# Three mixers of a transformer: the exact rest of each weight computed on GpSimd instead of VectorE

## The chip, the cores and the metric

One core of one Trainium2 chip runs the whole program. The metric is the device time of one execution in microseconds; of several executions of a kernel the median is taken. TensorE (PE) multiplies matrices, VectorE (DVE), ScalarE (ACT) and GpSimd (POOL) work on tiles elementwise, and SyncE (SP) and GpSimd start transfers from HBM.

## The reference

Two transformer blocks on 256 tokens of width 1024, all in float32. What is computed around the change is the hybrid mixer, run twice (once for each layer of the first block), and a third mixer with sparse attention, a state-space branch and memory attention in the second block:

```python
def hybrid_mixer(x, w_in, mix_scale, w_out, ...):
    proj = jnp.einsum('btd,de->bte', x, w_in)
    (a_q, a_k, a_v, a_decay, a_beta, a_gate, c_glu, f_q, f_k, f_v, f_forget) = split_columns(proj, IN_SIZES)
    ...
    o_a = gated_delta_rule(heads(a_q, GDN_HEADS), heads(a_k, GDN_HEADS), heads(a_v, GDN_HEADS), log_decay, beta)
    ...

def gated_delta_rule(q, k, v, g, beta):
    '''Chunked gated delta rule.
    S_t = exp(g_t) * S_{t-1} (I - beta_t k_t k_t^T) + beta_t k_t v_t^T ;  o_t = S_t^T q_t
    ...

def first_block(x, ...):
    for l in range(DEPTH):
        mix = hybrid_mixer(x, w_in[l], ...)
        x = layer_norm(DEEPNORM_ALPHA * x + mix, ln_mix_g[l], ln_mix_b[l])
        if l % 2 == 0:
            ff = swiglu(x, ffn_w1[l // 2], ffn_w3[l // 2], ffn_w2[l // 2])
        else:
            ff = moe_swiglu(x, moe_router[l // 2], moe_w1[l // 2], moe_w3[l // 2], moe_w2[l // 2])
        x = layer_norm(DEEPNORM_ALPHA * x + ff, ln_ffn_g[l], ln_ffn_b[l])
    return x
```

The mixer joins three branches: the gated delta rule (a solve in each chunk of 64 tokens, then a scan over four chunks), a depthwise convolution of 31 taps over a gated unit with a norm and a sigmoid behind it, and a forgetting attention. Their outputs are scaled, joined to 1024 columns and multiplied by `w_out`.

## The kernel before, in words

Seven stages run one after the other: mixer 1 (layer 0), a dense feed-forward, mixer 2 (layer 1, the same code), a mixture of experts, a feed-forward, mixer 3 (the second block's mixer), and a last feed-forward. A stage opens its PSUM banks with `banks(...)`, whose tags name how many banks each use has. The three mixers, and they alone, have the tags `a=2, g=4, f=2`.

Dense products are made of three fast matmuls instead of one slow one. `load` (line 162) has SP bring 128 x 2048 raw weights into one of four buffers. `part` (line 169) cuts them into parts of 1024 columns. For each part ACT writes the rounded half `wh` (line 172), and VectorE the exact rest `wl`, raw minus rounded (line 174). Each has three buffers. `mm3` (lines 182 to 185) multiplies high by high, high by low and low by high. A part feeds 24 matmuls in the mixers. `proj_a` and `proj_b` are the two forms of projection, with the activations on one side or the other; in the trace their outputs are `a_pA`, which reads `wl` in line 185, and `a_pB`, which reads it in line 184. A raw buffer is free for the next load once both halves are made.

A scheduler that simulates the program's times sets the order of the instructions on all engines; each engine then works through its own list in order. In a mixer, code written later has lower priority. After the projections that the gated delta rule needs come the inverse of the 16 x 16 blocks (`invert16`, lines 509 to 513, on VectorE), `invert32`, `solve`, the scan (line 713 is its subtraction on VectorE, lines 721, 728 and 730 its state), the attention `fox` (line 661 is the maximum over its scores, line 683 its output), the convolution and the gates, in the order of the call `self.emit(inverse(), scan(), fox(), conv(), gates())`. The generators are merged by the scheduler. `spare(c)` (line 612) makes a projection tile that one of them asks for.

The convolution `conv` (line 740) makes its gated input `cup` (line 748). It has two halves of 128 channels. In layer 0 six taps of each go to TensorE as matmuls with diagonal weights (`a_conv`, 12 in all), and the other 25 to VectorE, where the first is a multiplication (line 762) and the rest are 48 multiply-adds (line 764) in the tile `ccv`. The trace counts a float32 matmul as two. Line 765 adds both. Then come a mean (`f_cmean`), a variance (`f_cvar`), the norm (lines 771 to 781), the sigmoid, and line 803, which splits the result for the output projection `w_out`. That projection is made in four column blocks, each over all 1024 rows, and the rows of the convolution are the fourth and fifth eighth of the first block already. Line 792 makes the gate, lines 812 to 816 the norm of the scan's output, line 278 the split of the other rows, line 826 the sum with the residual.

GpSimd only starts transfers before the change (28 instructions in all), such as the constants at the start and the two rows of each norm (`load_rows`, line 286).

Of the kernel before, what the change touches and what calls it, by code (L numbers as in the profile page):

```python
# [9 lines left out]
F32 = mybir.dt.float32  # L10
# [5 lines left out]
ALU = mybir.AluOpType  # L16
# [87 lines left out]
class Net:  # L104
# [64 lines left out]
    def part(self, raw, o=0, m=1024):  # L169
        nc = self.nc  # L170
        wh = self.wp.tile([P, 1024], F32R, name="wh")
        nc.scalar.activation(wh[:, :m], raw[:, o:o + m], AF.Copy)  # L172
        wl = self.wp.tile([P, 1024], F32R, name="wl")
        nc.vector.tensor_tensor(wl[:, :m], raw[:, o:o + m], wh[:, :m].bitcast(F32), op=ALU.subtract)  # L174
        return wh[:, :m], wl[:, :m]

    def weights(self, src, n=2048):
# [9 lines left out]
    @contextmanager  # L187
    def banks(self, **tags):

        with self.tc.tile_pool(name="ps", bufs=1, space=bass.MemoryType.PSUM, reuse_waits="tile") as pool:  # L190
            self.pp, self.tags = pool, tags
            yield

    def ps(self, tag, name):
# [1714 lines left out]
```

## Time and profile before

| what | value |
|---|---|
| median of 3 runs | 2217.02 us |
| the runs | 2215.6, 2217.02, 2223.44 us |
| the profiled execution | 2220.2 us |
| its span in the profile | 2218.4 us |
| mean granted TensorE clock | 0.963 |
| busy share of the span | PE 93%, DVE 58%, ACT 46%, POOL 1% |

The profile is one execution. Busy time is the union of an engine's instructions. "Wait" rows name the instruction that came last before the engine went on. Windows count from the start of the span, and the granted clock of a window is a share of full speed (2.4 GHz). The stages stand at 0 to 201 us (mixer 1), 201 to 430 (feed-forward), 430 to 634 (mixer 2), 634 to 1600 (mixture of experts), 1600 to 1786 (feed-forward), 1786 to 2012 (mixer 3) and from 2012 (last feed-forward). A name such as `wl<-raw,wh` is the tile written and the tiles read.

### The profile page before, as it was taken

To read this page: it belongs to the slowest core of one execution; us is meant where nothing else is said; L and a number is where in the kernel's file an instruction comes from. 1 tells how busy PE (TensorE), PEld (TensorE's weight loads), DVE (VectorE), ACT (ScalarE), POOL (GpSimd) and SP (SyncE) were. 2 spreads that over 40 slices of the span, in tenths; PEclk is the share of its full clock that TensorE was granted. 3 is DMA by queue.
4 is the path that set the end of the run, shared out by engine and by line. 5 is a ranking of instruction groups with operands and counts; after the bars stand their busy time and mean duration, and the time that the engine had idled before them with its cause. 6 is when DMAs were issued, how large, how long until landed. Compare 5 with 4: busy or idle time off the path is not lost. (4 is left out here: it accounts for less than half of the span.)

```text
span 2218.4 us, 31878 instructions
## 1 busy us (share of the span) xinstructions
PE 2061.1 (93%) x12770; PEld 1609.1 (73%) x12770; DVE 1294.1 (58%) x1903; ACT 1023.4 (46%) x1448; POOL 14.6 (1%) x28
## 2 busy tenths in 40 slices
PE   8998959899979999998899999988699999999998
PEld 7878949788768888533368786332599988878997
DVE  6768925567659898410178985000554568665454
ACT  6545414465437777400167774000444444554443
POOL 0000000000000000000000000000000000000000
PEclk9979979999789999999999999999799999999999
DMA  6313797433158999799999999999555553344552
GB/s 231 105 39 135 213 105 292 160 115 106 72 214 315 350 346 349 307 425 425 426 425 425 355 343 358 425 425 424 193 178 187 188 196 128 133 150 153 184 188 96
DMA packets 80059, 548.31 MB, mean 247 GB/s; under 512 B 9392, under 2 KB 11696, under 8 KB 15008
## 3 DMA queue, kind: packets, MB, share of 16 engines
q1 hardware_dynamic: 75888, 527.40, 63.0%
q0 software_dynamic: 4016, 18.79, 4.2%
q8 instruction: 103, 1.69, 0.3%
q14 instruction: 52, 0.43, 0.1%
HBM read 536.72 MB, written 9.43 MB: 246 GB/s over the span
## 5 line engine op out<-in xcount | busy, mean ns | idle before, releaser
L174 DVE TENSOR_TENSOR wl<-raw,wh 128x1024 fp32r<-128x1024 f32 (+1 forms) x662 | 798.8, 1218 | 411.8 <-ACT wh L172 408.5
L172 ACT ACTIVATE wh<-raw 128x1024 fp32r<-128x1024 f32 (+1 forms) x662 | 693.9, 1055 | 629.9 <-PE a_pA L184 255.2
L183 PE MATMUL a_pA<-xTh,wh 128*128 128x256 f32 x1456 | 419.8, 289 | 26.0 <-ACT wh L172 22.3
L185 PE MATMUL a_pA<-xTh,wl 128*128 128x256 f32 x1456 | 416.0, 286 | 1.2 <-DVE wl L174 1.2
L184 PE MATMUL a_pA<-xTl,wh 128*128 128x256 f32 x1456 | 415.9, 286 | 0.0
L183 PEld LDWEIGHTS a_pA<-xTh,wh 128*128 128x128 f32 x1456 | 281.4, 194 | 34.8 <-ACT wh L172 23.2
L184 PEld LDWEIGHTS a_pA<-xTl,wh 128*128 128x128 f32 x1456 | 281.4, 193 | 4.5 <-issue 3.2
L185 PEld LDWEIGHTS a_pA<-xTh,wl 128*128 128x128 f32 x1456 | 281.1, 193 | 4.5 <-issue 2.2
L1032 PE MATMUL a_up<-raw,xef 128*64 128x512 f32 x896 | 218.7, 597 | 26.2 <-DMA raw<-in_moe_w_dram 26.2
L1037 DVE TENSOR_TENSOR mos<-mos,a_up 128x512 f32<-128x512 f32 x42 | 28.7, 682 | 267.4 <-PE a_up L1032 258.5
L184 PE MATMUL a_up<-wl,xeh 128*128 128x512 f32 x448 | 180.3, 402 | 1.9 <-DVE wl L174 1.8
L1032 PEld LDWEIGHTS a_up<-raw,xef 128*64 128x64 f32 x896 | 68.5, 136 | 154.8 <-issue 106.2
L185 PE MATMUL a_up<-wh,xel 128*128 128x512 f32 x448 | 178.0, 397 | 0.0
L183 PE MATMUL a_up<-wh,xeh 128*128 128x512 f32 x448 | 175.7, 399 | 0.0
L183 PE MATMUL a_pB<-wh,xTh 128*128 128x256 f32 x480 | 140.8, 295 | 5.7 <-ACT glu L620 3.2
L1065 PE MATMUL y_y<-raw,mof 128*64 128x512 f32 x448 | 133.4, 608 | 7.4 <-DMA raw<-in_moe_w_dram 7.3
L185 PE MATMUL a_pB<-wh,xTl 128*128 128x256 f32 x480 | 138.3, 291 | 1.5 <-DVE xTl L278 1.5
L184 PE MATMUL a_pB<-wl,xTh 128*128 128x256 f32 x480 | 139.2, 291 | 0.0
L184 PEld LDWEIGHTS a_up<-wl,xeh 128*128 128x128 f32 x448 | 84.7, 189 | 28.3 <-DVE wl L174 6.8
L1036 ACT ACTIVATE mos<-a_up 128x512 f32<-128x512 f32 x42 | 24.7, 587 | 170.8 <-PE a_up L1032 168.6
L184 PE MATMUL acc_acc<-wl,ffh 128*128 128x512 f32 x264 | 102.9, 395 | 0.5 <-DVE wl L174 0.5
L185 PE MATMUL acc_acc<-wh,ffl 128*128 128x512 f32 x264 | 102.7, 395 | 0.0
(559 smaller groups left out, 2772.2 us busy)
## 6 DMA issues: line engine op xcount, KB each, us to landing
raw<-in_moe_w_dram SPq DMA_DIRECT2D x336, 1024.0 KB, 10.6
raw<-in_ffn_in_dram SPq DMA_DIRECT2D x44, 1024.0 KB, 4.9
raw<-in_ffn_w_dram SPq DMA_DIRECT2D x33, 1024.0 KB, 5.0
raw<-in_w_in_a_dram SPq DMA_DIRECT2D x24, 1024.0 KB, 4.9
raw<-in_ffn_out_dram SPq DMA_DIRECT2D x22, 1024.0 KB, 4.9
raw<-in_w_out_dram SPq DMA_DIRECT2D x12, 1024.0 KB, 4.9
raw<-in_w_in_g_dram SPq DMA_DIRECT2D x12, 1024.0 KB, 5.0
raw<-in_w_in_b_dram SPq DMA_DIRECT2D x6, 1024.0 KB, 5.0
```

Of the source, the lines that this page charges most:

```text
L172: nc.scalar.activation(wh[:, :m], raw[:, o:o + m], AF.Copy)
L174: nc.vector.tensor_tensor(wl[:, :m], raw[:, o:o + m], wh[:, :m].bitcast(F32), op=ALU.subtract)
L183: mm(out, lh, rh, start=start, stop=False, skip_group_check=True)
L184: mm(out, lh, rl, start=False, stop=False, skip_group_check=True)
L185: mm(out, ll, rh, start=False, stop=stop, skip_group_check=True)
L1032: PE.matmul(ps[r], xe[0][:, k0, r], w[:, k * 512:k * 512 + 512], start=k0 == 0, stop=k0 == 7, skip_group_check=True)
L1036: self.last = S.activation(s, pp[0], AF.Silu)
L1037: V.tensor_tensor(s, s, pp[1], op=ALU.mult)
L1065: PE.matmul(py[h][r], hf[:, k, r], w[:, j * 1024 + h * 512:j * 1024 + h * 512 + 512], start=b == 0 and k == 0, stop=b == 6 and k == 3, ski ...
```

## The change

In the three mixers the subtraction of line 174 is issued on GpSimd instead of VectorE. The engine is chosen when the banks are opened: a stage with the tag `f` takes GpSimd, and the others keep VectorE. 123 of the 662 subtractions move: 34 in mixer 1 (one of 144 columns), 34 in mixer 2 (one of 144) and 55 in mixer 3 (one of 544). One line is added, so all lines behind 191 have a number higher by one.

```diff
         wl = self.wp.tile([P, 1024], F32R, name="wl")
-        nc.vector.tensor_tensor(wl[:, :m], raw[:, o:o + m], wh[:, :m].bitcast(F32), op=ALU.subtract)
+        self.rest.tensor_tensor(wl[:, :m], raw[:, o:o + m], wh[:, :m].bitcast(F32), op=ALU.subtract)
         return wh[:, :m], wl[:, :m]
...
         with self.tc.tile_pool(name="ps", bufs=1, space=bass.MemoryType.PSUM, reuse_waits="tile") as pool:
             self.pp, self.tags = pool, tags
+            self.rest = self.nc.gpsimd if "f" in tags else self.nc.vector
             yield
```

The scheduler then sets another order on every engine. On GpSimd, the start of the program, mixer 1 and the beginning of mixer 2 read as follows (`memd`, `biasd`, `rot` and `kept` are transfers of the feed-forward stage; `rows` are those of the norms):

```order
L174 ISA
L174 TENSOR_TENSOR wl<-raw,wh 128x144
L174 TENSOR_TENSOR wl<-raw,wh 128x1024 x28
L287 DMA rows<-in_ln_mix_dram 128x2048
L1366 DMA mem<-in_mem_dram 128x2048
L1387 DMA rb<-in_rel_bias_dram 32x8
L1388 DMA bk<-in_buckets_dram 32x512
L174 TENSOR_TENSOR wl<-raw,wh 128x1024 x5
...
L174 TENSOR_TENSOR wl<-raw,wh 128x144
L174 TENSOR_TENSOR wl<-raw,wh 128x1024
L287 DMA rows<-in_ln_ffn_dram 128x2048
```

The subtractions stand between the transfers that GpSimd issued before: the loads for the next stage are behind 29 of mixer 1's, and the load of the norm's rows in mixer 2 is behind the first two. In front of the first subtraction stands one instruction of another kind.

VectorE before, in mixer 1, from the attention's second half to the convolution's sum (`late` and `old` are the scan's tiles, `fsx` the attention's):

```order
L764 SCALAR_TENSOR_TENSOR ccv<-cup,p_72,ccv 128x256 x2
L730 COPY late<-g_S 64x3x64 x2
L764 SCALAR_TENSOR_TENSOR ccv<-cup,p_72,ccv 128x256 x2
L721 TENSOR_TENSOR old<-late,eg 64x192 x2
L764 SCALAR_TENSOR_TENSOR ccv<-cup,p_72,ccv 128x256 x5
L713 TENSOR_TENSOR late<-late,g_ws 64x384
L764 SCALAR_TENSOR_TENSOR ccv<-cup,p_72,ccv 128x256 x2
L174 TENSOR_TENSOR wl<-raw,wh 128x1024
L764 SCALAR_TENSOR_TENSOR ccv<-cup,p_72,ccv 128x256 x2
```

and with the change, in the same mixer, around the scan's third and last subtraction (line 714 now):

```order
L749 TENSOR_TENSOR cup<-glu 128x2x256
L714 TENSOR_TENSOR late<-late,g_ws 64x384
L763 TENSOR_SCALAR ccv<-cup,p_72 128x256 x2
L765 SCALAR_TENSOR_TENSOR ccv<-cup,p_72,ccv 128x256 x18
L684 TENSOR_TENSOR mixed<-f_fo,fsx 128x384
L765 SCALAR_TENSOR_TENSOR ccv<-cup,p_72,ccv 128x256 x21
L793 TENSOR_TENSOR gate<-gate,late 128x768
L765 SCALAR_TENSOR_TENSOR ccv<-cup,p_72,ccv 128x256 x3
L813 TENSOR_REDUCE ors<-late 128x6
```

Before, the multiply-adds of the convolution stood in twos and threes between the steps of the attention and the scan, and 28 of them were ahead of the scan's first copy (line 730); now all 48 follow its last subtraction. Six more stand behind the rows shown, mixed with lines 813 to 817.

TensorE with the change, at the end of the scan in mixer 1 (`g_ws` and `g_o` belong to the scan, `a_pB` is a projection, `a_conv` the convolution's matmuls):

```order
L363 MATMUL g_ws<-late 64x128 x3
L363 MATMUL g_o<-late,kq_283 64x128
L363 MATMUL g_o<-late,kq_358 64x128
L363 MATMUL g_o<-late,kq_431 64x128
L363 MATMUL a_conv<-cup,dgt 128x256 x2
L183 MATMUL a_pB<-wh,xTh 128x256
L184 MATMUL a_pB<-wl,xTh 128x256
L185 MATMUL a_pB<-wh,xTl 128x256
```

The first two of the twelve convolution matmuls come here, behind the scan's last `g_ws`; before, the first two stood ahead of the solve's end and nine of the twelve ahead of the scan's first `g_ws`. Of the 600 projection matmuls ahead of the convolution's mean, 33 now stand behind the scan's end, none before, and when the solve begins 451 have been issued, against 532 before. Of the attention's 18 last products (`f_fo`), twelve now stand behind the scan's last subtraction. Mixer 2 has the same pattern. In mixer 3 the attention's and the state-space's steps stand some 20 to 130 projection matmuls earlier, and the gates' projections stay last.

## Rows read from the trace of the kernel before

**Rows 1.** The page, part 1: busy us, share of the span, instructions.
```profile
PE 2061.1 (93%) x12770; PEld 1609.1 (73%) x12770; DVE 1294.1 (58%) x1903; ACT 1023.4 (46%) x1448; POOL 14.6 (1%) x28
```
**Rows 2.** The page, part 5: costliest groups (busy, mean ns | idle before, releaser).
```profile
L174 DVE TENSOR_TENSOR wl<-raw,wh 128x1024 fp32r<-128x1024 f32 (+1 forms) x662 | 798.8, 1218 | 411.8 <-ACT wh L172 408.5
L172 ACT ACTIVATE wh<-raw 128x1024 fp32r<-128x1024 f32 (+1 forms) x662 | 693.9, 1055 | 629.9 <-PE a_pA L184 255.2
```
**Rows 3.** Windows of the mixers: stretch, length, busy of each engine, granted clock, DMA share.
```profile
0.00:179.00 179.00, 162.69 (x1486) 138.37 (x1487) 125.22 (x306) 96.36 (x207) 4.82 (x12) 0.92 0.35 128
...
430.00:616.00 186.00, 166.65 (x1514) 140.41 (x1513) 130.68 (x304) 97.59 (x211) 0.53 (x1) 0.91 0.30 105
616.00:634.00 18.00, 17.74 (x148) 17.53 (x147) 10.41 (x16) 4.38 (x5) 0.00 (x0) 1.00 0.84 314
1786.00:2012.00 226.00, 217.40 (x1469) 187.16 (x1469) 163.11 (x261) 110.92 (x195) 1.59 (x3) 0.97 0.44 153
```
**Rows 4.** Windows, line 174 alone: length, busy of VectorE, granted clock, DMA share.
```profile
0.00:179.00 179.00, 34.40 (x29) 0.92 0.35 128
...
1786.00:2012.00 226.00, 66.19 (x55) 0.97 0.44 153
```
**Rows 5.** TensorE's waits, 0 to 179 us: total us, times, longest.
```profile
PE g_tr L267 <- DMA call<-in_consts_dram: 6.6, 1, 6.6
PE g_tr L267 <- DVE mixed L816: 2.3, 2, 1.4
...
PE a_pA L183 <- ACT wh L172: 1.2, 1, 1.2
```
**Rows 6.** Windows, slices of mixer 1 (columns: PE, PEld, DVE, ACT, POOL, clock).
```profile
60.00:72.00 12.00, 10.42 (x80) 8.65 (x80) 11.96 (x29) 3.74 (x6) 0.00 (x0) 1.00 0.27 89
...
120.00:126.00 6.00, 6.00 (x16) 3.30 (x15) 2.42 (x8) 2.35 (x9) 0.00 (x0) 0.50 0.00 0
...
138.00:144.00 6.00, 6.00 (x59) 4.33 (x58) 3.33 (x10) 2.25 (x9) 0.00 (x0) 0.52 0.01 3
144.00:150.00 6.00, 6.00 (x52) 5.51 (x53) 5.09 (x14) 3.51 (x10) 0.00 (x0) 1.00 0.00 0
...
168.00:174.00 6.00, 2.78 (x18) 1.72 (x16) 5.47 (x14) 3.50 (x10) 1.76 (x3) 1.00 0.13 23
```
**Rows 7.** VectorE's groups from 76 to 166 us (busy, mean ns | idle before).
```profile
L764 DVE SCALAR_TENSOR_TENSOR ccv<-cup,p,ccv 128x256 f32<-128x256 f32 x48 | 20.6, 476 | 0.2
L174 DVE TENSOR_TENSOR wl<-raw,wh 128x1024 fp32r<-128x1024 f32 x12 | 14.7, 1221 | 5.3 <-ACT wh L172 5.3
...
L661 DVE TENSOR_REDUCE fsx<-f_fl 128x2 f32<-128x256 f32 (+3 forms) x8 | 3.6, 451 | 13.0 <-PE f_fl L362 13.0
L713 DVE TENSOR_TENSOR late<-late,g_ws 64x384 f32<-64x384 f32 x3 | 1.7, 554 | 1.3 <-PE g_ws L362 1.3
```
**Rows 8.** VectorE's timeline in mixer 1 (start us, us, instruction).
```profile
162.31 0.67 DVE L765 TENSOR_TENSOR ccv<-ccv,a_conv 128x512 f32<-128x512 f32 x1
...
165.66 0.56 DVE L713 TENSOR_TENSOR late<-late,g_ws 64x384 f32<-64x384 f32 x1
...
177.57 0.88 DVE L803 SCALAR_TENSOR_TENSOR xTl<-ccv,msc,xTh 128x256 fp32r<-128x256 f32 x2 [0.58 <-ACT xTh L802]
```
**Rows 9.** TensorE's groups from 108 to 178 us.
```profile
L362 PE MATMUL a_conv<-cup,dgt 128*128 128x256 f32 x24 | 10.0, 540 | 0.0
...
L362 PE MATMUL f_fo<-fv,fpT 128*128 128x64 f32 x36 | 4.4, 278 | 0.0
```
**Rows 10.** Timeline of the start: VectorE's first subtraction, and TensorE's first use of it.
```profile
7.11 0.29 DVE L174 TENSOR_TENSOR wl<-raw,wh 128x144 fp32r<-128x144 f32 x1
...
10.54 0.32 PE L185 MATMUL a_pS<-xTh,wl 128*18 128x256 f32 x1
```
**Rows 11.** Timeline, start of mixer 2: VectorE, then TensorE.
```profile
428.73 1.23 DVE L174 TENSOR_TENSOR wl<-raw,wh 128x1024 fp32r<-128x1024 f32 x1 [3.10 <-ACT wh L172]
...
440.02 4.05 PE L267 MATMUL g_tr<-call,x 128*128 128x128 f32 x16 [9.70 <-DVE x L851]
```
**Rows 12.** Transfers: issues, KB each, median us from issue to landing.
```profile
rows<-in_ln_mix_dram POOLq DMA_DIRECT2D x2, 1024.0 KB, 6.2
```
**Rows 13.** The chain of waits of mixer 3, share of 1786 to 2012 us by line.
```profile
by line: PE a_pB L185 14.1%; PE a_pB L183 14.1%; PE a_pB L184 14.1%; PE g_al L1465 4.6%; PE a_pA L184 4.5%; PE a_pA L185 4.5%; PE a_pA L183 4.4%; PE f_bu L1465 3.8%; DVE wl L174 3.1%; PE f_ssy L1465 2.7%; PE f_br L183 2.3%; PE g_tr L267 2.2
```

## The prediction

> **What bounds the kernel now.** I read the page's busy shares first, then the costliest groups, then the windows by stage, then TensorE's waits, and last the slices and the order of the rows inside one mixer. TensorE is busy 93% of the span [rows 1]. The subtraction that is moved is the largest group of VectorE, 662 instructions and 798.8 us, but VectorE then idles 411.8 us more waiting for ACT's rounded part, and ACT in turn waits mostly for TensorE's last use of an old part [rows 2]: the chain of weights runs in step with TensorE, one 1024-wide part per 24 matmuls. At the pace of a full stretch, 17.74 us for 148 matmuls [rows 3], or 0.12 us each, TensorE needs 2.88 us for a part. VectorE needs 1.22.
>
> The three mixers are the stages that change: 0 to 201 us, 430 to 634 and 1786 to 2012. TensorE is busy 162.69 of 179, 166.65 of 186 and 217.40 of 226 us there; VectorE 125.22, 130.68 and 163.11 [rows 3]. The moved instruction is 34.40 us of VectorE in the first of these windows and 66.19 in the third [rows 4]. So the relief is large, some 27% and 41% of VectorE's work, but it is relief of an engine that is not the bound. In the first mixer TensorE's waits are headed by the first load, 6.6 us, and by the gated output, 2.3 us; where it waits in the chain of weights the releaser is ACT's part, 1.2 us [rows 5], and no row of that view names the subtraction. The slices say where TensorE still loses time: 1.6 us of twelve at 60 to 72 us, where VectorE is busy 11.96 of 12, and 3.2 of six at 168 to 174, in front of the output projection. They also show a granted clock of 0.50 to 0.52 in four slices from 120 to 144 us, the 1.2 GHz level, and 1.00 again from 144 [rows 6].
>
> **The change part by part.** *Moved.* 123 subtractions go to GpSimd: 34, 34 and 55. No row of before shows GpSimd computing on such a tile, so its time is bounded. The low end is ACT's 1.06 us for the same width; the high end is 2.88 us, above which GpSimd would be TensorE's pace in dense stretches. I take 2 x 1.22 = 2.44 us, the VectorE row once for each of its two inputs. With three buffers a part is prepared two parts ahead, 5.8 us; ACT's 1.06 and 2.44 fit. So TensorE doesn't wait for the slower subtraction in steady state, and I cost it at nothing there; at 5 us a part the cover is gone and the 55 parts of mixer 3 would cost some 2 us each. The Trainium skill, "GPSIMD Engine Reference", section 3.1, gives a tensor_tensor at twice the width as 4497 ns on GpSimd and 2293 on VectorE, a ratio of 1.96; an estimate from it is 2.2 to 2.4 us, and the sum by it would be the same.
>
> *Start.* The first narrow subtraction ran at 7.11 us and TensorE used it at 10.54 [rows 10]. On GpSimd it stands behind four DMA issues that are done before then, and a row of its own of the first use. Bounds 0 and +6 (the time TensorE idles at the start anyway [rows 5]); I take +3.
>
> *What moves with it in mixers 1 and 2.* The order of all engines changes, and this is the main term. Before, the 48 multiply-adds of the depthwise convolution, 20.6 us of VectorE [rows 7], were spread over the attention and the scan, in gaps where VectorE waited 13.0 us for the attention's scores [rows 7]. Now they stand in one block behind the last subtraction of the scan, and their twelve matmuls and 33 projection matmuls behind the scan too. Behind the block stand the mean, the variance, the sigmoid, and then the output projection, which needs the result in its first quarter.
>
> The scan's last subtraction was at 165.66 us, and the last input of the output projection came at 177.57 [rows 8]: 12 us of tail. The new tail is the 48 multiply-adds, 20.6, and eleven instructions among them at the 0.55 us of the scan's row [rows 7], 6.1: 26.7 us. From the sum with the matmuls' part (162.31) to the last input (177.57) it took 15.3 us [rows 8], in which VectorE did six scan and gate instructions that now come earlier, 6 x 0.55 = 3.3: 12.0. New tail 38.7 us, so **+26.7**.
>
> Against it, the scan's end comes earlier, because it is TensorE's queue that sets it: the engine is busy 6.00 of 6 us in the slices from 120 to 150 us [rows 6]. Work leaves the front of it: the convolution's matmuls, 10.0 us, and two thirds of the attention's last products, 4.4 x 2/3 = 2.9 [rows 9], and 33 projections x 0.12 = 4.0. Together **-16.9**. TensorE's waits for a full VectorE are at least the 1.6 us of [rows 6]; I take **-2**. The slow clock: without the 10.0 us of the convolution, some 14 of the 24 us at 0.50 remain; at full clock they would take half. Bounds 0 and -7, and I take the middle, **-3**, since more projection matmuls now stand in this stretch. After an idle tail the clock starts low, as the 0.50 rows show: **+1**, bounds 0 and +3. Per mixer: 26.7 - 16.9 - 2 - 3 + 1 = +5.8, within -1 and +13.
>
> *Mixer 2's start.* The load of the norm's two rows is issued on GpSimd; it now stands behind a full subtraction whose input is ready when VectorE's began, 428.73 us [rows 11]. With 2.44 and the 6.2 us of such a load [rows 12] it lands at 437.4 or a little later, 2.6 us before TensorE's transposes begin at 440.02 [rows 11], and between the two stand three or four instructions of the norm: +1, bounds 0 and +3. In mixer 1 the same load and three more stand between the subtractions of the output projection; the three parts in front cover 3 x 2.88 us.
>
> *Mixer 3.* TensorE is busy 217.40 of 226 us, so at most 8.6 can go. The chain of waits has the subtraction at 3.1% of this stage, 7.0 us [rows 13]. Its place is taken by GpSimd's, which is longer but earlier; I take half, **-3**, bounds -8 and +3.
>
> Sum: +3 + 2 x 5.8 + 1 - 3 = **+12.6 us**, or 13. The profiled execution took 2220.2 us, 3.2 more than the median of 2217.02; against the median the forecast is **2230 us**.
>
> **The rivals.** *The block is paid for (no change).* The scan ends 25.9 us earlier, not 21.9: full clock through the solve (-7), and the start and the clock of the projection cost nothing. Then each of the first two mixers stands at 26.7 - 25.9, about +1, and mixer 3 gives 5: 2214 us. For it: the slow stretch is real, and more large matmuls now stand in it. Against it: the empty tail lowers the clock again where the output projection starts.
>
> *VectorE was the bound before the solve (faster).* VectorE is full at 60 to 72 us [rows 6], and 17 subtractions (29 of [rows 4] less the 12 of [rows 7]) stand in front of 76 us, where the inverse begins: 20.7 us. If that chain and not TensorE's queue sets the solve, the scan ends 16.9 + 20.7 = 37.6 us sooner, 11 more than the tail costs; two mixers give -22, mixer 3 -5 and the start +3: 2193 us. It decides if TensorE idles while VectorE is full; the 1.6 us of twelve are the whole of that in the slice read, which speaks against it.
>
> *GpSimd and VectorE hold each other up (slower still).* If a VectorE instruction with two SBUF inputs waits for a running GpSimd subtraction, the multiply-adds and the inverse lose up to 2.44 us for each of GpSimd's. In the tail two or three parts are prepared, +6, and in front of the scan as much VectorE time is lost as was won, so the -2 goes: 8 us per mixer, and mixer 3's -3 becomes +2: 13 + 16 + 5 = +34, or 2251 us. No row of before has both engines computing at once, so nothing here excludes it. The Trainium skill, "SBUF — State Buffer", section "Who interferes with whom", states such an exclusive lock between the two engines; no run here shows it yet.
>
> That the change doesn't do what it says is excluded for the place of the instructions: GpSimd's order has all 123.
>
> **How the numbers follow.** A measurement of this kernel can tell about 0.5% from no change, 11 us: 2206 to 2228 is "same". Forecast, 0.40: own range 2218 to 2242, of which 0.27 lies above 2228 and 0.13 within. Block paid for, 0.25: 0.20 within, 0.05 faster. VectorE the bound, 0.15: faster. Lock, 0.20: slower. So faster 0.20, same 0.33, slower 0.47. The range leaves out half of the fastest case and the upper part of the lock: 2200 to 2256.
>
> **What would show it.** In the profile after: a GpSimd row for the subtraction near 2.4 us; the scan's last subtraction of mixer 1 near 165.7 - 16.9 - 2 - 3 + 3 = 147 us; the multiply-adds in one run of 20 to 27 us behind it with TensorE mostly idle and waiting for the convolution's sum; the output projection at full pace from some 186 us instead of 178. Multiply-adds longer than 0.48 us each, or gaps between them at GpSimd's subtractions, would show the lock. The forecast is wrong if the scan ends well before 147 or at its old place, or if TensorE waits for the subtraction more than 5 us in a stage.

## The result and the profile after

| what | before | after |
|---|---|---|
| median, both kernels measured side by side | 2217.97 us (4 runs) | 2325.41 us (4 runs) |
| lowest and highest | 2215.6, 2223.44 us | 2322.99, 2327.38 us |
| the profiled execution | 2220.2 us | 2323.83 us |
| mean granted TensorE clock | 0.963 | 0.941 |

The ratio is 1.0475, with the interval 1.0445 to 1.0505: 107 us slower, where 13 were forecast and the range ended at +39. The profiled execution grew by 103.6 us. By stage: mixer 1 ends at 232.24 us, where it ended at 198.88 (+33.4); mixer 2, from its first transposes to its last sum, takes 233.0 us, where it took 193.8 (+39.3); mixer 3 takes 255.0, where it took 226.2 (+28.8). The other stages together make +2. So the whole loss lies in the three stages that were changed, and each loses about as much as the others.

The page's busy shares (part 1) of the changed kernel, which answer to [rows 1]:

```profile
PE 2098.7 (90%) x12770; PEld 1639.5 (71%) x12770; DVE 1274.5 (55%) x1780; ACT 1023.4 (44%) x1448; POOL 308.4 (13%) x151
```

and the two groups of the subtraction among its costliest groups (part 5; busy us, mean ns of one | idle before, releaser), which answer to [rows 2]:

```profile
L174 DVE TENSOR_TENSOR wl<-raw,wh 128x1024 fp32r<-128x1024 f32 x539 | 651.9, 1222 | 339.3 <-ACT wh L172 336.9
...
L174 POOL TENSOR_TENSOR wl<-raw,wh 128x1024 fp32r<-128x1024 f32 (+2 forms) x123 | 293.9, 2399 | 725.3 <-ACT wh L172 719.3
```

Two numbers that don't fit together are the first finding. VectorE's subtractions fell from 798.8 to 651.9 us, by 146.9. VectorE as a whole fell from 1294.1 to 1274.5, by 19.6. The other 127.3 us came back as longer instructions of the same count. GpSimd takes some 2.4 us for a part of 1024 columns, twice VectorE's time.

TensorE's row splits the 103.6 us in another way. It ran the same 12770 matmuls and was idle for 223.3 us of its span, where it had been idle for 157.3 (+66.0); the matmuls themselves took 2098.7 us, where they had taken 2061.1 [rows 1] (+37.6). This second part goes with the lower granted clock, 0.941 for 0.963. So over a third of the loss is not a wait but slower matmuls; what lowered the clock was not separated.

The windows of the three mixers (stretch, length, busy of PE, PEld, DVE, ACT, POOL, then the granted clock), beside [rows 3]:

```profile
0.00:234.00 234.00, 193.91 (x1650) 167.56 (x1650) 146.67 (x301) 106.55 (x221) 84.41 (x46) 0.88 0.32 113
...
472.00:710.00 238.00, 204.95 (x1658) 176.43 (x1658) 133.80 (x275) 100.08 (x212) 74.56 (x32) 0.81 0.29 103
...
1858.00:2116.00 258.00, 225.81 (x1480) 191.81 (x1478) 143.78 (x209) 111.96 (x196) 135.09 (x59) 0.93 0.39 134
```

In mixer 1 TensorE is idle for 40 of 234 us, and its granted clock is 0.88. TensorE's waits from 0 to 234 us show for what it idles, beside [rows 5]:

```profile
PE g_tr L268 <- DVE mixed L817: 10.6, 2, 10.4
...
PE a_pB L183 <- ACT xTh L803: 6.4, 1, 6.4
PE g_lb L363 <- DVE sg L495: 4.7, 2, 2.6
PE g_x L363 <- DVE u L514: 3.8, 1, 3.8
```

Not one of these waits is for GpSimd. They are for VectorE's other work, or for ACT's step behind it: the convolution's result (`xTh`) and the gated output (`mixed`) in the tail, and the inverse (`sg`, `u`) ahead of the scan.

VectorE's timeline in mixer 1 (start us, us, instruction) shows both halves of the trouble. These rows belong beside [rows 8]:

```profile
62.79 2.40 DVE L605 SCALAR_TENSOR_TENSOR kq<-kq,eg 128x256 f32<-128x256 f32 x1
...
85.76 2.20 DVE L510 TENSOR_TENSOR w<-lb,x 128x60 f32<-128x60 f32 x1
...
88.28 0.20 DVE L511 TENSOR_REDUCE x<-w 128x12 f32<-128x60 f32 x1
...
117.90 2.05 DVE L663 SCALAR_TENSOR_TENSOR fsx<-fsx,cum 128x2 f32<-128x2 f32 x1
...
166.86 0.56 DVE L714 TENSOR_TENSOR late<-late,g_ws 64x384 f32<-64x384 f32 x1
...
168.11 7.21 DVE L765 SCALAR_TENSOR_TENSOR ccv<-cup,p,ccv 128x256 f32<-128x256 f32 x18
...
175.96 12.65 DVE L765 SCALAR_TENSOR_TENSOR ccv<-cup,p,ccv 128x256 f32<-128x256 f32 x21
...
195.75 0.68 DVE L766 TENSOR_TENSOR ccv<-ccv,a_conv 128x512 f32<-128x512 f32 x1
...
209.50 0.89 DVE L804 SCALAR_TENSOR_TENSOR xTl<-ccv,msc,xTh 128x256 fp32r<-128x256 f32 x2 [0.57 <-ACT xTh L803]
```

GpSimd's timeline beside the first three stretched ones:

```profile
62.52 2.39 POOL L174 TENSOR_TENSOR wl<-raw,wh 128x1024 fp32r<-128x1024 f32 x1 [2.60 <-ACT wh L172]
...
85.50 2.39 POOL L174 TENSOR_TENSOR wl<-raw,wh 128x1024 fp32r<-128x1024 f32 x1 [0.63 <-ACT wh L172]
...
117.59 2.34 POOL L174 TENSOR_TENSOR wl<-raw,wh 128x1024 fp32r<-128x1024 f32 x1 [4.30 <-ACT wh L172]
```

An instruction on two columns takes 2.05 us, and it ends at 119.95, when GpSimd's subtraction ends (119.93). The one on 60 columns ends at 87.96, GpSimd's at 87.89. Each met a running subtraction and was done within 0.3 us of its end. The second half is the order: the multiply-adds now stand behind the scan, whose end did not come earlier. Its last subtraction is at 166.86 us, where it was at 165.66 [rows 8] and 147 was forecast. From there to the last input of the output projection it takes 42.6 us, where it took 12.

### The profile page after: what moved, and what is told of

Its sections match the earlier page's. It is cut to its first block, busy times and chain, and to the rows that moved or that the text cites. A ratio compares the mean times of both kernels' runs of the same rounds, so it can differ in the third digit from the quotient of the medians.

```text
span 2322.0 us, 31938 instructions
## 1 busy us (share of the span) xinstructions
PE 2098.7 (90%) x12770; PEld 1639.5 (71%) x12770; DVE 1274.5 (55%) x1780; ACT 1023.4 (44%) x1448; POOL 308.4 (13%) x151
## 5 line engine op out<-in xcount | busy, mean ns | idle before, releaser
L174 DVE TENSOR_TENSOR wl<-raw,wh 128x1024 fp32r<-128x1024 f32 x539 | 651.9, 1222 | 339.3 <-ACT wh L172 336.9
L183 PE MATMUL a_pA<-xTh,wh 128*128 128x256 f32 x1456 | 426.2, 293 | 24.2 <-ACT wh L172 20.5
L185 PE MATMUL a_pA<-xTh,wl 128*128 128x256 f32 x1456 | 422.1, 290 | 2.6 <-DVE wl L174 2.6
L174 POOL TENSOR_TENSOR wl<-raw,wh 128x1024 fp32r<-128x1024 f32 (+2 forms) x123 | 293.9, 2399 | 725.3 <-ACT wh L172 719.3
L183 PEld LDWEIGHTS a_pA<-xTh,wh 128*128 128x128 f32 x1456 | 286.1, 197 | 32.9 <-ACT wh L172 21.7
L185 PEld LDWEIGHTS a_pA<-xTh,wl 128*128 128x128 f32 x1456 | 285.8, 196 | 6.7 <-DVE wl L174 3.5
L184 PEld LDWEIGHTS a_pA<-xTl,wh 128*128 128x128 f32 x1456 | 286.4, 197 | 4.6 <-issue 3.3
L183 PEld LDWEIGHTS a_pB<-wh,xTh 128*128 128x128 f32 x480 | 97.2, 203 | 14.5 <-ACT xTh L803 11.4
```

The costliest lines, as they stand in the source:

```text
L174: self.rest.tensor_tensor(wl[:, :m], raw[:, o:o + m], wh[:, :m].bitcast(F32), op=ALU.subtract)
L183: mm(out, lh, rh, start=start, stop=False, skip_group_check=True)
L184: mm(out, lh, rl, start=False, stop=False, skip_group_check=True)
L185: mm(out, ll, rh, start=False, stop=stop, skip_group_check=True)
```

## The experiments

Two theories were set against each other. By the one, the loss is the new **order**: the convolution's block at the end of the mixers. By the other, it is **contention**: VectorE's instructions are held while GpSimd subtracts. A third was that the subtraction on GpSimd is simply too slow for TensorE. In most runs the order of the instructions is pinned: a table gives the lists of TensorE, VectorE, ACT and SP, and adds no wait. It is not pinned in `change_again` and in the two `conv_ahead` runs. The kernel before ran beside them on the same chip (medians 2222.35, 2220.03, 2215.26 and 2221.24 us in the four series).

### The two halves by themselves

`old_order_gpsimd`: the rest is made on GpSimd, while TensorE, ACT and SP keep the order of before and VectorE keeps it for what is left to it.

```diff
-        nc.vector.tensor_tensor(wl[:, :m], raw[:, o:o + m], wh[:, :m].bitcast(F32), op=ALU.subtract)
+        self.rest.tensor_tensor(wl[:, :m], raw[:, o:o + m], wh[:, :m].bitcast(F32), op=ALU.subtract)
...
+            self.rest = self.nc.gpsimd if "f" in tags else self.nc.vector
...
+        net.pin()
```

> The subtraction of the mixers is on GpSimd as in the change, but TensorE, VectorE, ACT and the load queue issue everything else in exactly the order of the kernel before (issue order alone is pinned; no wait is added). The change took 107 us more than before. If the new order made the loss (the convolution's block behind the scan), this run is within 15 us of the kernel before. If GpSimd and VectorE hold each other up, most of the loss stays: 60 to 110 us over before, with VectorE instructions of two SBUF inputs stretched to as much as 2.4 us. If both matter about equally, 40 to 60 us.

Measured: 2262.77 us, ratio 1.0188 (1.0143 to 1.0234), +40. The mixers grew by 18.0, 6.5 and 18.9 us. Its shares on the page:

```profile
PE 2076.7 (92%) x12770; PEld 1621.8 (72%) x12770; DVE 1275.0 (56%) x1780; ACT 1023.9 (45%) x1448; POOL 309.0 (14%) x151
```

VectorE's total is the same 1275 us as in the change: the relief is lost in the old order too. So contention alone makes some 40 us, with no order to blame: the lower edge of what was expected if both theories hold.

`new_order_vector`: every engine in the change's order, the rest on VectorE as before.

```diff
+        net.pin()
```

> The subtraction stays on VectorE as before, and all other instructions of TensorE, VectorE, ACT and the load queue stand in the order that the change brought. If the order made the loss: 70 to 110 us over before. If the engines' interference made it: at most 25 us over before, most of it in mixers 1 and 2 (my forecast's price of the convolution's tail was 12 us in all), none in mixer 3; the multiply-adds of the convolution stay at 0.48 us each.

Measured: 2278.0 us (2269.19 and 2286.82), ratio 1.0257 (1.0155 to 1.0359), +56, between the 25 and the 70 of the two theories; in the profiled execution, the faster one, the mixers grew by 22.1, 16.1 and 10.3 us. VectorE's timeline there:

```profile
157.26 0.56 DVE L803 TENSOR_TENSOR late<-late,g_ws 64x384 f32<-64x384 f32 x1
...
184.77 0.68 DVE L855 TENSOR_TENSOR ccv<-ccv,a_conv 128x512 f32<-128x512 f32 x1
...
198.32 0.89 DVE L893 SCALAR_TENSOR_TENSOR xTl<-ccv,msc,xTh 128x256 fp32r<-128x256 f32 x2 [0.58 <-ACT xTh L892]
```

The tail is 41.1 us, near the 38.7 of the forecast. But even with no contention the scan ends only 8.4 us earlier (157.26 for 165.66), not 18.9. The windows show where the rest went:

```profile
36.00:48.00 12.00, 11.49 (x66) 8.72 (x66) 5.79 (x11) 6.95 (x19) 0.00 (x0) 0.58 0.23 84
48.00:60.00 12.00, 12.00 (x69) 10.49 (x69) 5.45 (x8) 9.04 (x18) 0.00 (x0) 0.71 0.25 89
...
96.00:108.00 12.00, 9.01 (x227) 8.58 (x229) 9.63 (x22) 2.60 (x3) 0.00 (x0) 0.92 0.34 119
...
120.00:132.00 12.00, 12.00 (x156) 10.49 (x156) 2.23 (x9) 5.87 (x24) 0.00 (x0) 0.73 0.19 80
132.00:144.00 12.00, 12.00 (x76) 9.21 (x74) 3.96 (x10) 1.89 (x7) 0.00 (x0) 0.86 0.00 0
```

The slow stretch of [rows 6] shrank (0.73 and 0.86 for 0.50), but another came: the granted clock is 0.58 and 0.71 from 36 to 60 us, with TensorE busy 11.49 and 12.00 of 12 us there and 11.93 of the 12 before. The kernel before has 1.00 in all three slices. And from 96 to 108 us, among 227 small matmuls, TensorE idles 3 us, while before it had no idle time in any slice from 96 to 156 us.

### What holds VectorE up

In these runs VectorE makes every rest as before, in the pinned order of before, and GpSimd does something more that nobody reads. What such a run loses is due to GpSimd's work alone.

`spare_sub_gpsimd`: GpSimd makes the same rests a second time, in pieces of 512 columns.

```diff
+        if "f" in self.tags:
+            for a in range(0, m, 512):
+                b = min(m, a + 512)
+                nc.gpsimd.tensor_tensor(self.idle[:, :b - a], raw[:, o + a:o + b], wh[:, a:b].bitcast(F32), op=ALU.subtract)
```

> The kernel before, order pinned, VectorE still makes every rest. In the mixers GpSimd makes it a second time, in two pieces of up to 512 columns into a tile that nobody reads. No relief, no new order, no result that anyone waits for. Interference theory: VectorE instructions with two SBUF inputs are stretched by the rest of a piece (about 1.2 us each time), VectorE's own subtraction among them, and the time rises by 40 to 110 us. If GpSimd and VectorE don't hold each other up: within 5 us of before.

Measured: 2316.9 us, 1.0432 (1.0388 to 1.0476), +95. VectorE's and GpSimd's groups:

```profile
L249 DVE TENSOR_TENSOR wl<-raw,wh 128x1024 fp32r<-128x1024 f32 (+1 forms) x662 | 852.0, 1299 | 392.3 <-ACT wh L247 389.2
```
```profile
L253 POOL TENSOR_TENSOR idle<-raw,wh 128x512 f32<-128x512 f32 (+1 forms) x244 | 414.8, 1700 | 622.8 <-ACT wh L247 517.5 <-issue 88.8 <-POOL idle L253 2.2
```

Both engines lose: a piece of 512 columns takes 1.70 us, where the one part of 544 columns in the change took 1.39, and VectorE's own subtractions grew by 53 us (852.0 for 798.8) among 146 us more busy time.

`spare_half_gpsimd`: the same with one piece for each part, half of the work.

```diff
-            for a in range(0, m, 512):
+            for a in range(0, min(m, 512), 512):
```

> As the run with the spare subtraction, with one piece of 512 columns to a part instead of two. If each piece costs its own wait: half of the 95 us, 35 to 60. If what costs is only the length of the longest wait in the chain of the delta rule: nearer 95. The mean piece shorter than 1.7 us would show that the two engines queue for each other less.

Measured: 2253.78 us, 1.0161 (1.0124 to 1.0199), +34: about a third of 95, not a half, and just under the 35 to 60 expected. The loss grows faster than the work. The pieces did not become shorter, as they would if the two engines queued for each other less: they took 1.88 us in the mean, for 1.70.

`spare_set_gpsimd`: as many instructions, but GpSimd reads one column, so that it still waits for the part, and then only writes.

```diff
-                nc.gpsimd.tensor_tensor(self.idle[:, :b - a], raw[:, o + a:o + b], wh[:, a:b].bitcast(F32), op=ALU.subtract)
+                nc.gpsimd.tensor_copy(self.idle[:, :1], wh[:, a:a + 1].bitcast(F32))
+                nc.gpsimd.memset(self.idle, 0.0)
```

> As the run with the spare subtraction, but each piece is a copy of one column (which waits for the rounded part) and a memset of 512 columns, which reads nothing. If it is GpSimd's reading of SBUF beside VectorE that holds them up: within 10 us of before, no stretched VectorE instruction. If any GpSimd instruction that writes SBUF does it: a rise in proportion to GpSimd's busy time, compared with the run with the spare subtraction.

Measured: 2226.02 us, 1.0019 (0.9992 to 1.0047), no change, though GpSimd is busy 290.1 us, nearly as long as in the change. GpSimd's groups:

```profile
L253 POOL COPY idle<-wh 128x1 f32<-128x1 f32 x244 | 145.9, 598 | 647.0 <-ACT wh L247 633.6 <-ACT nhsq L374 2.5 <-ACT memss L374 0.9
L254 POOL MEMSET idle<- 128x512 f32 x244 | 129.7, 532 | 14.4
```

A busy GpSimd, its semaphores and its writes cost nothing that can be measured; its reads do.

`spare_copy_gpsimd`: the piece is copied, one input read instead of two.

```diff
-                nc.gpsimd.tensor_tensor(self.idle[:, :b - a], raw[:, o + a:o + b], wh[:, a:b].bitcast(F32), op=ALU.subtract)
+                nc.gpsimd.tensor_copy(self.idle[:, :b - a], wh[:, a:b].bitcast(F32))
```

> As the run with the spare subtraction, but GpSimd's spare piece is a copy of the rounded part: one input read from SBUF instead of two. The rule of the Trainium skill's page SBUF, that a GpSimd instruction that reads SBUF holds up a VectorE instruction with two SBUF inputs, has no number of inputs in it: by it the loss is that of the spare subtraction in proportion to GpSimd's busy time (50 to 100 us). If two reading ports were needed: within 10 us.

Measured: 2230.65 us, 1.0056 (1.0031 to 1.0081), +12. VectorE was busy 32 us longer in all (1326.5 us, for 1294.1 before), and a copy took 1.04 us in the mean. The number expected for "any read" was missed: one input instead of two costs an eighth, not a half. That a copy's single read holds VectorE up too is shown; why a second input costs so much more is not.

### The tail by itself

`tail_vector`: rest on VectorE, order of before; only the multiply-adds of the convolution, and the mean that needs them, move behind the scan's last subtraction.

```diff
-                    V.tensor_tensor(ut[r, t, :], ut[r, t, :], pv[r, :384], op=ALU.subtract)
+                    last = V.tensor_tensor(ut[r, t, :], ut[r, t, :], pv[r, :384], op=ALU.subtract)
+                    self.scan_end = last.ins
...
+            with self.tc.issue_after(self.scan_end):
```

> VectorE makes every rest, and the order is that of the kernel before, except that in mixers 1 and 2 the convolution's multiply-adds on VectorE are queued behind the scan's last subtraction, and what follows them is left to the scheduler. This is the tail of the new order without its earlier scan. The forecast's term for the tail was 26.7 us a mixer, so 40 to 55 us over before in all if nothing else in VectorE's queue was held up by the multiply-adds. If the new order's loss came from the projections that moved and the slow clock, and the tail is covered, under 20 us.

Measured: 2267.91 us, 1.0225 (1.0188 to 1.0262), +48. VectorE's timeline:

```profile
162.01 0.56 DVE L805 TENSOR_TENSOR late<-late,g_ws 64x384 f32<-64x384 f32 x1
...
170.00 15.13 DVE L858 SCALAR_TENSOR_TENSOR ccv<-cup,p,ccv 128x256 f32<-128x256 f32 x38
185.16 0.69 DVE L859 TENSOR_TENSOR ccv<-ccv,a_conv 128x512 f32<-128x512 f32 x1
...
199.09 0.88 DVE L897 SCALAR_TENSOR_TENSOR xTl<-ccv,msc,xTh 128x256 fp32r<-128x256 f32 x2 [0.58 <-ACT xTh L896]
```

The tail is 37.1 us, for 12 before, and mixer 1 ends 21.4 us later. The forecast's main term, 26.7 for each of two mixers or 53, stands. Clearing the block from the front of VectorE's list, with TensorE's list left as it was, brought the scan's end 3.7 us forward.

### Repeats, and versions that might win

`new_order_vector_again` and `change_again` put the halves beside the change on one chip.

> The same program as new_order_vector, whose two times were 47 and 65 us over the kernel before, for an interval. Order and interference add up to the change's 107 us if it is 60 to 65; at 45 to 50 some 14 to 19 us of the change are an interaction, GpSimd's subtractions falling into the convolution's block.

> The change itself on the same chip as the three others: 100 to 112 us over before. Only as their reference.

Measured: 2281.84 us, 1.0282 (1.0221 to 1.0343), +67; and 2325.96 us, 1.0499 (1.0468 to 1.0529), +111. So GpSimd costs 44 us on top of the new order and 40 on top of the old one. The two halves add up, as far as the new order's own spread (2269 to 2296 us over both series) lets one say so: 56 to 67 for the order, 40 to 44 for contention, 107 to 111 together. The spread lies for the most part in mixer 2: the profiled execution of `new_order_vector` took 209.9 us there at a granted clock of 0.90, that of `new_order_vector_again` 225.5 us at 0.81, with the same program. So by stage the sum holds only roughly. In mixer 2 the order cost 16.1 or 31.7 us and contention 6.5, for 39.3 together; in mixer 1 it was 22.1 or 24.7 and 18.0, for 33.4 together.

`w_out_gpsimd`: in the old order, GpSimd only for the 16 parts of the output projections in mixers 1 and 2, where VectorE has little else to do.

```diff
+            self.rest = self.nc.vector
...
+            self.rest = self.nc.gpsimd
...
+            self.rest = self.nc.vector
```

> The order of the kernel before, and GpSimd makes the rest only for the output projections of mixers 1 and 2, 16 parts, where VectorE's other work reads one input from SBUF and one from PSUM, or is a statistic of one input. By the rule there is nothing to hold up there but the loads' and memory stage's few instructions: 2215 to 2227 beside a kernel before of 2217 to 2222, within 0.3%. If any GpSimd subtraction costs what it cost in the change on average, 107 us for 123, it would be 14 us slower.

Measured: 2217.24 us, 1.0001 (0.9975 to 1.0027): free, and no gain. The 14 us that 16 parts would cost at the change's average are excluded. That VectorE reads few pairs of SBUF tiles there was the reason expected; it was not tested by itself.

`conv_ahead_gpsimd`: the change, with the convolution given a higher priority than the scan, behind the attention's projections. `conv_ahead_vector` is the same edit with the rest on VectorE.

```diff
-        self.emit(inverse(), scan(), fox(), conv(), gates())
+        f = fox()
+        self.emit(inverse(), (next(f) for _ in FOXC), conv(), scan(), f, gates())
```

> The change, with the convolution ahead of the scan in the order of the code (inverse, the attention's projections, convolution, scan, the rest of the attention, gates), so that its 48 multiply-adds stand ahead of the scan and there is no tail behind it. If tail and interference are separate causes, the tail's part goes (about 48 us) and what stays is the interference, 40 to 65 us over before. If the block only moves the wait to another place: 90 us or more over before.

> The kernel before with the same edit; VectorE makes every rest. If the place of the multiply-adds is worth something in the kernel before too, where the output projection waits about 12 us behind the scan's last subtraction in each of two mixers: up to 10 us faster. If the multiply-adds ahead of the scan hold up the inverse and the solve: 20 us slower or more (48 of 0.43 us).

Measured: 2298.29 us, 1.0353 (1.0313 to 1.0392), +77; and 2224.43 us, 1.0008 (0.9982 to 1.0034), no change. VectorE's timeline of the first:

```profile
122.17 17.62 DVE L765 SCALAR_TENSOR_TENSOR ccv<-cup,p,ccv 128x256 f32<-128x256 f32 x39
...
166.32 0.56 DVE L714 TENSOR_TENSOR late<-late,g_ws 64x384 f32<-64x384 f32 x1
166.91 0.48 DVE L805 SCALAR_TENSOR_TENSOR xTl<-ccv,msc,xTh 128x256 fp32r<-128x256 f32 x1
```

The tail is gone: the convolution's result is ready with the scan's last subtraction. With VectorE the edit costs nothing, where up to 10 us of gain or 20 and more of loss had been expected. But the two runs differ in more than the engine. The order was not pinned here, and with the rest on GpSimd the scheduler set another one: 39 multiply-adds stand in one block ahead of the scan there, while on VectorE they stand mostly in twos between the steps of the inverse, the solve and the scan, at most eight together:

```profile
120.72 3.21 DVE L764 SCALAR_TENSOR_TENSOR ccv<-cup,p,ccv 128x256 f32<-128x256 f32 x8
```

The 74 us between them are therefore contention and another order together, and this pair doesn't separate them. The 77 us also hold mixer 3, which the edit doesn't touch and which takes 255.2 us, as long as in the change, where 10.3 of its 28.8 are the order. So the 77, though beyond the 40 to 65 expected, don't contradict the 40 to 44 of the pinned pairs. In VectorE's groups of this run the product `old<-late,eg` of the scan takes 1094 ns where it took 350, so that stretched instructions now stand on the scan's own chain. No version was faster than the kernel before.

## Why the prediction was wrong

**Right.** The sign had the largest chance (slower, 0.47). The subtraction on GpSimd was taken at 2.44 us, and the 120 wide ones of `old_order_gpsimd` take 2442 ns. TensorE was not to wait for it; its waits name it in none of mixers 1 and 2, and with 0.9 us in mixer 3. The new tail was worked out as 38.7 us and measured 41.1 with the order alone and 42.6 with the change. The term of +26.7 for each of two mixers is 53; made by itself it measured 48.

**The start, +3**, was 0: GpSimd's first subtraction stands at 6.48 us and TensorE uses it at 10.47, for 10.54 before [rows 10]. **Mixer 2's start, +1**, held within its bounds of 0 to 3: VectorE waits 0.37 us for the rows, and the feed-forward stage before is some 3 us longer.

**The step that failed first is the credit for an earlier end of the scan**: "Work leaves the front of it", -16.9, with -2 for waits and -3 for the clock. It took the slices of [rows 6] from 120 to 150 us, where TensorE is busy throughout, to speak for the whole front of the mixer. With the order alone, the scan ended 8.4 us earlier. TensorE idled some 15.4 us up to 156 us, where it had idled 11.1 (+4.2 for the -2), and at the lower clock it lost 3.3 us more, not 3 less, since a second slow stretch appeared at 36 to 60 us. (The loss of a slice of 6 us is its length times one minus its clock, added up over the slices.) The two turns, 6.2 and 6.3 us, are 12.5 of the 13.5 that were missing from 21.9. So the work that left the queue was worth some 16 us, near its price of 16.9; what failed is that TensorE's waits and its slow stretches would shrink with it. The price was made from matmuls that leave; what the same queue would wait for once they had left was never asked. With GpSimd the remaining 8.4 us went as well, and 1.2 more: the scan ends 9.6 us later than in `new_order_vector`. The term of +1 for a low clock behind the tail pointed at the rows of 0.50, but in these TensorE is busy 6.00 of 6 us, so they don't show what an idle engine brings. Behind the new tail the clock was indeed low: 0.67 and 0.72 in `new_order_vector` from 180 to 204 us, where TensorE was busy 7.57 and 5.67 of 12.

**The second is the chance and the price of the rival in which the two engines hold each other up.** It had 0.20 and +21 over the forecast. It is the other half of the result, 40 to 44 us. The price counted 8 us in a mixer: what VectorE had won in front of the scan, and two or three parts of the tail. VectorE's groups from 60 to 200 us of mixer 1 show how wide it is:

```profile
L765 DVE SCALAR_TENSOR_TENSOR ccv<-cup,p,ccv 128x256 f32<-128x256 f32 x48 | 23.9, 563 | 0.0
...
L510 DVE TENSOR_TENSOR w<-lb,x 128x24 f32<-128x24 f32 (+14 forms) x15 | 13.7, 912 | 2.4 <-ACT lb L499 2.0
...
L605 DVE SCALAR_TENSOR_TENSOR kq<-kq,eg 128x256 f32<-128x256 f32 x3 | 4.6, 1532 | 0.0
...
L511 DVE TENSOR_REDUCE x<-w 128x12 f32<-128x24 f32 (+14 forms) x15 | 4.0, 264 | 0.4
...
L663 DVE SCALAR_TENSOR_TENSOR fsx<-fsx,cum 128x2 f32<-128x2 f32 (+1 forms) x8 | 3.2, 397 | 0.2
...
L482 DVE SCALAR_TENSOR_TENSOR NT<-g_kk,E 128x128 f32<-128x128 f32 x6 | 1.7, 279 | 0.1
```

Before, the same groups had 476, 268, 411, 262, 147 and 280 ns, the inverse this:

```profile
L509 DVE TENSOR_TENSOR w<-lb,x 128x24 f32<-128x24 f32 (+14 forms) x15 | 4.0, 268 | 1.2 <-ACT lb L498 1.0
```

The tail's multiply-adds, for which the +6 was meant, lost only 3.3 us. The inverse (line 510, fifteen small products) lost 9.7, and it stands on the chain to the solve; `u` and `sg`, for which TensorE now waits 8.5 us, are of that chain. What the stretched rows share is that they read two tiles of SBUF: the reduction (one input) and line 482, which reads PSUM beside one tile of SBUF, kept their times. The Trainium skill, "SBUF — State Buffer", section "Who interferes with whom", says that a VectorE instruction with two SBUF inputs contends with a GpSimd instruction that reads SBUF and not with one that only writes, and that the loser blocks for the whole instruction. The trace agrees: two columns took 2.05 us and ended with GpSimd's subtraction, and the write-only run stood at 1.0019. Two inputs are not the only case, though. VectorE's groups of the change have conversions and scalings of a single tile that were stretched as well, from 186 and 748 ns before (and 187 and 750 in `new_order_vector`):

```profile
L134 DVE CAST maskb<-call 128x64 bf16<-128x64 f32 x4 | 7.2, 1864 | 0.0
L1374 DVE TENSOR_SCALAR mem<-mem,memss 128x1024 f32<-128x1024 f32 x2 | 5.8, 2918 | 0.4 <-ACT memss L295 0.4
```

The prediction named the rule of the two inputs and gave it a fifth, for want of a row; but a rule that names exactly the two kinds of instruction at hand should have had more.

**Mixer 3, -3, became +29.** "Longer but earlier" was right of the subtraction. But the order cost 10.3 us there and contention 18.9. The chain of waits of mixer 3 shows the place, the state-space scan:

```profile
1885.62 6.58 DVE bu L1542 x4
...
1914.11 4.50 DVE bu L1542 x4
...
1937.78 6.64 DVE bu L1542 x4
...
1964.92 6.69 DVE bu L1542 x4
```

These four instructions, which read two tiles, took 2.35 us before where the same four stood in that chain:

```profile
1843.69 2.35 DVE bu L1541 x4
```

TensorE's waits from 1858 to 2116 us with the change:

```profile
PE f_ssy L1466 <- DVE bu L1547: 18.0, 3, 7.5
```

No row of before has this wait. In `new_order_vector` it is 9.0 us: half of it is the order, half the stretching.

## What to carry to other kernels

Before handing elementwise work to GpSimd, count what runs on VectorE beside it, not the busy share that goes away. Here VectorE's instructions with two SBUF tiles as inputs, and some conversions and scalings of one, were held while GpSimd subtracted: 127 of 147 us came straight back, and on short instructions of the critical chain. An edit of one line can move a block of VectorE in front of the end of a stage: read where the block lands, and give a credit for the place that it left only after naming what the engine there waits for next. To tell contention from order, pin the order and add the work a second time where nobody reads it; two versions that the scheduler orders by itself, like the `conv_ahead` pair, don't tell them apart.

## What the runs showed that was not expected

GpSimd loses as well: a piece of 512 columns took 1.70 to 1.88 us beside a busier VectorE, where 544 columns took 1.39 in the change. One-input instructions were stretched too, a conversion of 64 columns to ten times its time. One and the same program took 209.9 us in mixer 2 at a granted clock of 0.90, and 225.5 at 0.81. The cost is far from proportional to GpSimd's busy time: +34 us for one piece of a part and +95 for two, +12 for copies, nothing for writes alone.
